# Zero products in TensorE's waits, tile ends on ScalarE, first weights in parts and gate rows a tile sooner, in an encoder layer

## Chip, core and metric

The kernel runs on one core of one Trainium2 chip. The metric is the time of one execution on the device in microseconds (us). The engines are TensorE (PE in rows: matrix products; PEld: its weight loads), VectorE (DVE), ScalarE (ACT), GpSimd (POOL) and SyncE (SP). Each runs its own queue of instructions in order. SP's queue issues the loads and POOL's queue the stores.

## What is computed

One layer of a hybrid encoder on 1024 tokens of 1024 channels, in fp32. The part that this change touches is the normalization, its modulation by `c`, and the projection to q and k:

```python
mod = jax.nn.silu(c) @ w_ada + b_ada
sh1, sc1, gt1, sh2, sc2, gt2 = jnp.split(mod[:, None, :], N_MOD, axis=-1)
h = rmsnorm(x, norm1_g) * (1.0 + sc1) + sh1
z = h @ w_in
u, v, q, k, va, gate_a, gate_b = jnp.split(z, cuts, axis=-1)
a_out = gmlp_branch(u, v, gm_v_g, gm_w_s, gm_b_s) @ w_a
b_out = window_attention_branch(q, k, va, q_norm_g, k_norm_g, attn_sink) @ w_b
merged = jax.nn.sigmoid(gate_a) * a_out + jax.nn.sigmoid(gate_b) * b_out
x = x + gt1 * (merged @ w_o)
h2 = rmsnorm(x, norm2_g) * (1.0 + sc2) + sh2
f_gate, f_up = jnp.split(h2 @ w_ffn_in, 2, axis=-1)
x = x + gt2 * ((jax.nn.silu(f_gate) * f_up) @ w_ffn_out)
```

## The kernel before

Every large product of two fp32 matrices is done as three products of split operands. A number is split into a high part (a cast to float32r, on ACT) and a low part (the number less its high part, on DVE); high by high, high by low and low by high are added up in PSUM. Weights come in units of 128 x 1024 (`raw`), whose parts are called `wh` and `wl`; three buffers of each rotate. `unit` loads one, casts it and takes the low part. The activations' parts are `hH` and `hL` (both `h` in rows).

The layer works on two halves of 512 tokens: `half(0)`, `half(1)`. Activations lie transposed, channels on the partitions, in 8 tiles of 128 channels (k = 0 to 7). Half 0 takes 640 columns, the 512 tokens and 128 more for the attention window (the halo).

*Half 0's begin* is written in program order (`in_order`), so each engine's queue follows the code. The 8 tiles of `xT` are loaded, then pair 0 of modulation rows (`ada_pair(k)`: the scale row SC1+k and the shift row SH1+k of tile k, 1 MB), then the first unit of `w_q` and of `w_kv`. Squares are taken on ACT and added up on DVE in `ss`; PE sums `ss` over the partitions (`total`), ACT takes the root, DVE the reciprocal (`rcol`), PE spreads it over the partitions in a bank (`spread`), and ACT copies the bank to `rb` (tile `ss` again). For each tile k the loop then does the following:

- DVE scales the tile by its scale column and `rb` (`x`, in rows `mid<-mid,mod,ss`).
- The shift end (`ada_end(SH1 + k)`) turns the dotted shift row into the column `sh`: one DVE operation on 128x1 (`mod<-acc_mod,cc`).
- ACT makes `hH` and the halo's high part and shifted copy, POOL the halo's low part (`mid<-mid,mid 128x128`).
- DVE dots the next tile's scale row with silu(c) (`ada_dot`, in rows `mid,acc_mod<-mid,silu_c`), makes `hL`, takes the scale end of the next tile (`mod<-acc_mod,badap,cc`) and dots the next shift row. POOL's queue stores the scaled tile (`x0d`).
- PE does 8 products of 512 columns for q with `hH` and 4 with `hL` (banks `mm`), and 10 and 5 of 256 columns for k (banks `at`).

A unit of `w_q` holds two tiles' weights and one of `w_kv` four. At each odd k below 7 the next `w_q` unit is loaded, cast and split; the second `w_kv` unit is loaded at k = 3 and split at k = 4. Behind the loop come the products for v. A scheduler sets the order of what is not `in_order`.

*Half 1* runs the same loop on activations that are ready (`h_next`) with its first units split ahead (`early`). In it the rows for the gates (GT1 and on) are brought in, each in two halves of 512 columns in the streams `hs` and `xs`: `ada_half_load` issues the loads on SP, `ada_half` dots both halves on DVE, takes the ends, and loads the next row.

Every operation recorded through the engines' wrapper has the line L76, every load L137.

## Time and profile before

| | |
|---|---|
| runs (us) | 1243.43, 1244.94, 1246.81; median 1244.94 |
| profiled execution | 1245.15 us, of which the span is 1243.3 |
| busy, of the span | PE 98%, PEld 81%, DVE 74%, ACT 46%, POOL 15% |
| granted TensorE clock, mean | 0.999 |
| idle time of PE before its column sums, for DVE's `ss` | 7.5 us, once |

The span is what the hardware profiler recorded from the first instruction to the last. A row of the timeline gives the start and the busy time in us, the engine, the line, the operation, what it writes and reads with the shape, a count of neighbours put together, and in brackets the idle time before it and what ended that. Rows of a sequence of instructions overlap a little, since an instruction starts before the one ahead has drained.

### The profile page before, as it was taken

Reading aid. Unit: us, or ns where it says so; the run is one execution under the profiler, and the core shown is the slowest. Engines: PE = TensorE matmul, PEld = TensorE weight load, DVE = VectorE, ACT = ScalarE, POOL = GpSimd, SP = SyncE. Lnnn points to the kernel's source line nnn. Section 1 sums busy time; section 2 is a strip of 40 time slices with the busy share of each in tenths; the row PEclk is TensorE's granted clock in tenths of the full one; section 3 lists DMA queues with packets and bytes.
Section 4 is the critical chain, followed back from the end, with each engine's and each line's share of the span. In section 5 each row is a group of like instructions: output and inputs, shape, how many; then the busy total and the mean of one; then the engine's idle time right before and its main releaser. Section 6 shows DMA issues by size and latency. Waiting matters only on the chain.

```text
span 1243.3 us, 15662 instructions
## 1 busy us (share of the span) xinstructions
PE 1220.3 (98%) x5634; PEld 1010.6 (81%) x5634; DVE 914.7 (74%) x1548; ACT 577.3 (46%) x938; POOL 183.6 (15%) x233
## 2 busy tenths in 40 slices
PE   6999999999999999999999999999999999999998
PEld 4888888888887787888888888888888887888887
DVE  8997884487898798966797766666766666665746
ACT  5467864267876333534554333333333335433341
POOL 1223430023432001322100001010000000010001
PEclk9999999999999999999999999999999999999999
DMA  9622258431157457777503445455554459896642
GB/s 367 254 102 81 74 193 289 145 102 52 51 174 237 164 190 251 282 261 255 201 34 119 174 149 202 153 194 200 188 212 160 170 195 376 318 349 231 199 153 102
DMA packets 77664, 236.29 MB, mean 190 GB/s; under 512 B 9361, under 2 KB 9361, under 8 KB 71570
## 3 DMA queue, kind: packets, MB, share of 16 engines
q1 hardware_dynamic: 55442, 143.00, 33.0%
q0 software_dynamic: 18688, 85.99, 19.4%
q10 hardware_dynamic: 3456, 6.29, 1.3%
q8 instruction: 44, 0.72, 0.2%
q14 instruction: 34, 0.28, 0.1%
HBM read 177.58 MB, written 57.67 MB: 189 GB/s over the span
## 4 chain that ended last, share of the span: by engine, by line
PE 71%; DVE 11%; issue 9%; DMA 4%; ACT 3%; POOL 0%; SPq 0%; ACTq 0%; DVEq 0%; POOLq 0%
PE mm L76 36%; PE at L76 35%; DVE mid L76 3%; DVE wl L76 2%; ACT wh L76 2%; DMA wo<-in_w_out_dram 1%; DMA wS<-wo 1%; DVE hs L76 1%; DMA raw<-in_w_ga_dram 1%; DMA xs<-x1sd 1%; DVE t L76 1%; DVE ws L76 1%; DVE xs L76 1%; DVE raw L76 1%; ACT lb L76 1%
## 5 line engine op out<-in xcount | busy, mean ns | idle before, releaser
L76 ACT CAST wh<-raw 128x1024 fp32r<-128x1024 f32 x155 | 162.3, 1051 | 145.0 <-PE at L76 44.5
L76 DVE TENSOR_TENSOR wl<-raw,wh 128x1024 fp32r<-128x1024 f32 x141 | 171.9, 1221 | 71.1 <-ACT wh L76 68.8
L76 PE MATMUL mm<-mid,wh 128*128 128x512 f32 x696 | 214.8, 390 | 0.3
L76 PEld LDWEIGHTS mm<-mid,wh 128*128 128x128 f32 x696 | 130.3, 188 | 28.0 <-DVE xs L76 0.6
L76 PE MATMUL at<-j,wh 128*128 128x512 f32 x464 | 143.0, 389 | 0.0
L76 PE MATMUL mm<-mid,wl 128*128 128x512 f32 x348 | 135.5, 389 | 0.5 <-POOL wl L76 0.5
L76 PE MATMUL mm<-wh,h 128*128 128x512 f32 x384 | 129.7, 399 | 1.9 <-ACT h L76 1.9
L76 PEld LDWEIGHTS at<-j,wh 128*128 128x128 f32 x464 | 86.9, 188 | 18.6 <-ACT wh L76 0.4
L76 DVE TENSOR_TENSOR wl<-ws,wh 128x1024 fp32r<-128x1024 f32 (+1 forms) x55 | 62.0, 1128 | 44.4 <-ACT wh L76 44.4
L76 PE MATMUL at<-j,wl 128*128 128x512 f32 x232 | 90.4, 390 | 0.5 <-DVE wl L76 0.5
L76 PE MATMUL mm<-j,wh 128*128 128x512 f32 x288 | 89.0, 390 | 0.3 <-ACT wh L76 0.3
L76 PE MATMUL at<-h,wh 128*128 128x512 f32 x288 | 88.9, 390 | 0.0
L76 PEld LDWEIGHTS mm<-wh,h 128*128 128x128 f32 x384 | 71.7, 189 | 16.7 <-ACT h L76 2.8
L76 PE MATMUL mm<-h,wh 128*128 128x512 f32 x272 | 84.6, 392 | 0.0
L76 ACT CAST wh<-ws 128x1024 fp32r<-128x1024 f32 (+1 forms) x55 | 53.6, 974 | 58.1 <-DVE ws L76 42.1
L76 PEld LDWEIGHTS mm<-mid,wl 128*128 128x128 f32 x348 | 65.3, 188 | 14.6 <-POOL wl L76 1.0
L76 PE MATMUL mm<-wl,h 128*128 128x512 f32 x192 | 76.0, 396 | 0.7 <-DVE wl L76 0.7
L76 PEld LDWEIGHTS mm<-j,wh 128*128 128x128 f32 x288 | 53.8, 188 | 11.7 <-ACT wh L76 0.7
L76 PEld LDWEIGHTS at<-h,wh 128*128 128x128 f32 x288 | 53.9, 188 | 11.1
L76 PEld LDWEIGHTS mm<-h,wh 128*128 128x128 f32 x272 | 50.6, 188 | 10.4
L76 ACT ACTIVATE xs<-xs 128x512 f32<-128x512 f32 x21 | 13.3, 632 | 96.8 <-DVE xs L76 96.8
L76 PE MATMUL mm<-j,wl 128*128 128x512 f32 x144 | 56.2, 390 | 0.5 <-DVE wl L76 0.5
(286 smaller groups left out, 2558.9 us busy)
## 6 DMA issues: line engine op xcount, KB each, us to landing
raw<-in_w_gate_dram SPq DMA_DIRECT2D x28, 512.0 KB, 5.1
tA<-hid POOLq DMA_DIRECT2D x11, 1024.0 KB, 4.9
tB<-hid POOLq DMA_DIRECT2D x11, 1024.0 KB, 4.9
wo<-in_w_out_dram POOLq DMA_DIRECT2D x22, 512.0 KB, 6.4
wS<-wo POOLq DMA_DIRECT2D x11, 1024.0 KB, 5.3
raw<-wS SPq DMA_DIRECT2D x44, 256.0 KB, 3.1
raw<-tB SPq DMA_DIRECT2D x44, 256.0 KB, 4.2
raw<-in_w_out_dram SPq DMA_DIRECT2D x33, 256.0 KB, 5.5
```

The source lines that it names most:

```text
L76: ins = f(*args, **kw)
```

## The change

It does four things.

- `warm(n)` issues n products of 128x512 of zeros into the first q bank, which the first real product starts afresh: 18 ahead of the column sums, 2 between these and the spread, 4 behind the openings of the k banks. The q banks are taken earlier for it.
- The loop's shift ends and scale ends go from DVE to ACT. A scale end is an activation there, with the gain as its scale and the new column `badg` (badap times the gain, one DVE operation of 128x8) as its bias. The scale end of tile 0 stays on DVE.
- The first units of `w_q` and `w_kv` are loaded in parts (512 and 512, 256 and 768 columns), with pair 1 between; casts and low parts are done in the same parts. Tile 0 is scaled in two parts straight from the spread's banks, and the copy to `rb` comes after `hH(0)`. The low part of each later `w_q` unit is taken at the even tile that needs it, after `x`, not at the odd tile before.
- Half 1 loads gate rows at k = 1 and 2 and dots them at k = 3 to 6, where it loaded at 2 and 3 and dotted at 4 to 7.

The order of PE's first instructions, before, from the column sums (`at<-ones,ss`) over the spread (`at<-ident,rcol`) and the openings of the k banks (`at<-identr,zeros`) to the first products:

```order
L76 MATMUL at_190<-ones,ss_167 128x1 x5
L76 MATMUL at_212<-ident,rcol_122 128x128 x4
L76 MATMUL at_218<-ident,rcol_122 128x128
L76 MATMUL at_229<-identr,zeros 128x512
L76 MATMUL at_230<-identr,zeros 128x512
L76 MATMUL mm_225<-wh_202,h_221 128x512
L76 MATMUL mm_225<-wl_203,h_221 128x512
```

And PE's after the change, from just behind the products of `crow`:

```order
L76 MATMUL mm_196<-identr,zeros 128x512 x18
L76 MATMUL at_218<-ones,ss_172 128x1 x5
L76 MATMUL mm_196<-identr,zeros 128x512 x2
L76 MATMUL at_239<-ident,rcol_123 128x128 x4
L76 MATMUL at_244<-ident,rcol_123 128x128
L76 MATMUL at_250<-identr,zeros 128x512
L76 MATMUL at_251<-identr,zeros 128x512
L76 MATMUL mm_196<-identr,zeros 128x512 x4
L76 MATMUL mm_196<-wh_230,h_246 128x512
L76 MATMUL mm_196<-wl_231,h_246 128x512
```

The products of zeros (`mm_196<-identr,zeros`) stand ahead of each of the three steps. DVE's order before, from the reciprocal to the `x` operation of tile 1:

```order
L76 RECIPROCAL rcol_122<-ms_196 128x5
L76 SCALAR_TENSOR_TENSOR mid_157,acc_mod<-mid_157,silu_c 128x1024
L76 TENSOR_TENSOR wl_203<-raw_159,wh_202 128x1024
L76 SCALAR_TENSOR_TENSOR mid_127<-mid_127,mod,ss_211 128x640
L76 TENSOR_SCALAR mod<-acc_mod,cc 128x1
L76 TENSOR_TENSOR wl_207<-raw_161,wh_206 128x1024
L76 SCALAR_TENSOR_TENSOR mid_209,acc_mod<-mid_209,silu_c 128x1024
L76 SCALAR_TENSOR_TENSOR h_223<-mid_127,mod,h_221 128x512
L76 SCALAR_TENSOR_TENSOR mod<-acc_mod,badap,cc 128x1
L76 SCALAR_TENSOR_TENSOR mid_209,acc_mod<-mid_209,silu_c 128x1024
L76 SCALAR_TENSOR_TENSOR mid_127<-mid_127,mod,ss_211 128x640
L76 TENSOR_SCALAR mod<-acc_mod,cc 128x1
```

DVE's after, over the same stretch, with `x` of tile 0 in parts from the banks (`at_239`, `at_244`):

```order
L76 RECIPROCAL rcol_123<-ms_224 128x5
L76 SCALAR_TENSOR_TENSOR mid_158,acc_mod<-mid_158,silu_c 128x1024
L76 SCALAR_TENSOR_TENSOR mid_128<-mid_128,mod,at_239 128x512
L76 TENSOR_TENSOR wl_231<-raw_160,wh_230 128x512
L76 SCALAR_TENSOR_TENSOR mid_128<-mid_128,mod,at_244 128x128
L76 TENSOR_TENSOR wl_234<-raw_161,wh_233 128x256
L76 SCALAR_TENSOR_TENSOR mid_164,acc_mod<-mid_164,silu_c 128x1024
L76 SCALAR_TENSOR_TENSOR h_248<-mid_128,mod,h_246 128x512
L76 SCALAR_TENSOR_TENSOR mid_164,acc_mod<-mid_164,silu_c 128x1024
L76 SCALAR_TENSOR_TENSOR mid_128<-mid_128,mod,ss_236 128x640
L76 TENSOR_TENSOR wl_231<-raw_160,wh_230 128x512
L76 TENSOR_TENSOR wl_234<-raw_161,wh_233 128x768
```

The operations of 128x1 are gone from DVE, the low part of wq stands behind the first part of `x`, and the second parts of both units stand behind `x` of tile 1. DVE's order in half 1 before, from the first gate row (`hs_2323`, `hs_2324`) to the low part of the second `w_q` unit (`wl_2278`); `wl_2244` is that of the first `w_kv` unit:

```order
L76 SCALAR_TENSOR_TENSOR hs_2323,acc_mod<-hs_2323,silu_c 128x512
L76 TENSOR_TENSOR wl_2201<-raw_2198,wh_2200 128x1024
L76 SCALAR_TENSOR_TENSOR hs_2324,part_2385<-hs_2324,silu_c 128x512
L76 TENSOR_TENSOR acc_mod<-acc_mod,part_2385 128x1
L76 TENSOR_SCALAR mod<-acc_mod,cc 128x1
L76 TENSOR_TENSOR wl_2244<-raw_2241,wh_2243 128x1024
L76 SCALAR_TENSOR_TENSOR xs_2356,acc_mod<-xs_2356,silu_c 128x512
L76 TENSOR_TENSOR wl_2278<-raw_2275,wh_2277 128x1024
```

And after; rows 1 (`xs_2335`, `xs_2336`) and 2 (`hs_2360`, `hs_2361`), the low part of the first `w_kv` unit now `wl_2277` and that of the second `w_q` unit `wl_2311`:

```order
L76 SCALAR_TENSOR_TENSOR xs_2335,acc_mod<-xs_2335,silu_c 128x512
L76 TENSOR_TENSOR wl_2234<-raw_2231,wh_2233 128x1024
L76 SCALAR_TENSOR_TENSOR xs_2336,part_2393<-xs_2336,silu_c 128x512
L76 SCALAR_TENSOR_TENSOR hs_2360,acc_mod<-hs_2360,silu_c 128x512
L76 TENSOR_TENSOR acc_mod<-acc_mod,part_2393 128x1
L76 SCALAR_TENSOR_TENSOR hs_2361,part_2427<-hs_2361,silu_c 128x512
L76 TENSOR_SCALAR mod<-acc_mod,cc 128x1
L76 TENSOR_TENSOR acc_mod<-acc_mod,part_2427 128x1
L76 TENSOR_SCALAR mod<-acc_mod,cc 128x1
L76 TENSOR_TENSOR wl_2277<-raw_2274,wh_2276 128x1024
L76 SCALAR_TENSOR_TENSOR xs_2398,acc_mod<-xs_2398,silu_c 128x512
L76 TENSOR_TENSOR wl_2311<-raw_2308,wh_2310 128x1024
```

Two gate rows instead of one stand ahead of the low part of the first `w_kv` unit, and row 3 stands where row 2 did.

The diff:

```diff
--- before.py
+++ after.py
@@ -183,6 +183,7 @@
     cc = const.tile([P, 72], F32, tag="cc", name="cc")
     bada, g1c, g2c, bsT = cc[:, :48], cc[:, 48:56], cc[:, 56:64], cc[:, 64:72]
     badap = const.tile([P, 48], F32, tag="badap", name="badap")
+    badg = small.tile([P, 16], F32, tag="badg", name="badg", bufs=1)
 
     def load_cond():
         crow = wpool.tile([P, UNIT], F32, tag="raw", name="crow")[0:1, :]
@@ -734,6 +735,14 @@
         koff = 0 if hf == 0 else NT - 1
 
 
+        def low(w, src, a, b):
+            V.tensor_tensor(w[1][:, a:b], src[:, a:b], w[0][:, a:b].bitcast(F32), op=ALU.subtract)
+
+        def warm(n):
+            for _ in range(n):
+                T.matmul(qps[0], zeros, identr.unsqueeze(1).to_broadcast([P, 4, P]), start=True,
+                         stop=True)
+
         if hf == 0:
             in_order[0] = True
             xt = [midt(F32, 1) for _ in range(3)]
@@ -746,7 +755,12 @@
             for k in range(KT):
                 load(xt[k], xT[k * P : (k + 1) * P, :640])
             r = ada_pair(0)
-            wq0, wk0 = raw_unit(w_q[0]), raw_unit(w_kv[0])
+            wq0, wk0 = (wpool.tile([P, UNIT], F32, tag="raw", name=nm("raw")) for _ in range(2))
+            load(wq0[:, :512], w_q[0][:, :512])
+            load(wk0[:, :256], w_kv[0][:, :256])
+            r1 = ada_pair(1)
+            load(wq0[:, 512:], w_q[0][:, 512:])
+            load(wk0[:, 256:], w_kv[0][:, 256:])
             cond = silu_rows(crow)
             ss = ss_tile()
             sqs = [midt(F32, 1)[:, 0, :] for _ in range(3)]
@@ -759,7 +773,10 @@
                 if k == 1:
                     silu_cond(cond)
                     V.tensor_scalar(badap, bada, 1.0, None, op0=ALU.add)
+                    V.tensor_tensor(badg[:, :8], badap[:, SC1 : SC1 + 8], g1c, op=ALU.mult)
                     build_bias(*base_bias, range(7, NH))
+            qps = [mm_bank() for _ in range(NT)]
+            warm(18)
             total = at_bank()
             for i in range(NT + 1):
                 T.matmul(total[:, i : i + 1], ss[:, i * P : (i + 1) * P], ones[:, 0:1], start=True,
@@ -770,25 +787,28 @@
             ada_end(SC1, g1c[:, 0:1])
             V.reciprocal(rcol[0], root)
             ada_dot(r[:, 1, :], SH1)
-            wq = unit(None, V, wq0)
+            wq = [wpool.tile([P, UNIT], F32R, tag=x, name=nm(x)) for x in ("wh", "wl")]
+            A.copy(wq[0][:, :512], wq0[:, :512])
             wk = [wpool.tile([P, UNIT], F32R, tag=x, name=nm(x)) for x in ("wh", "wl")]
-            A.copy(wk[0], wk0)
-            r = ada_pair(1)
+            A.copy(wk[0][:, :256], wk0[:, :256])
+            r = r1
             rb = ss_tile()
-            A.copy(rb[:, :HALF], spread(rcol[0], NT))
-            A.copy(rb[:, HALF:], spread(rcol[0][:, NT : NT + 1], 1))
+            warm(2)
+            bcs = spread(rcol[0], NT), spread(rcol[0][:, NT : NT + 1], 1)
             hH = [hid(), hid()]
             hL = [hid(), hid()]
         else:
             hH, hL = h_next
 
         nkv = NT + 1 - 2 * hf
-        qps = [mm_bank() for _ in range(NT)]
+        if hf == 1:
+            qps = [mm_bank() for _ in range(NT)]
         kbk = [at_bank() for _ in range(3)]
         if hf == 0:
             kps = [kbk[t // 2][:, (t % 2) * 256 : (t % 2 + 1) * 256] for t in range(nkv)]
             for t in range(2):
                 open_bank(kbk[t], identr, zeros)
+            warm(4)
         else:
             kps = [kbk[t][:, :256] for t in range(nkv)]
         for k in range(KT):
@@ -798,12 +818,28 @@
                 sh = mod[:, SH1 + k : SH1 + k + 1]
                 if 0 < k < KT - 1:
                     r = ada_pair(k + 1)
-                V.scalar_tensor_tensor(out=x, in0=x, scalar=mod[:, SC1 + k : SC1 + k + 1], in1=rb,
-                                       op0=ALU.mult, op1=ALU.mult)
-                ada_end(SH1 + k)
+                sc = mod[:, SC1 + k : SC1 + k + 1]
+                if k == 0:
+                    V.scalar_tensor_tensor(out=x[:, :HALF], in0=x[:, :HALF], scalar=sc, in1=bcs[0],
+                                           op0=ALU.mult, op1=ALU.mult)
+                    low(wq, wq0, 0, 512)
+                    V.scalar_tensor_tensor(out=x[:, HALF:], in0=x[:, HALF:], scalar=sc, in1=bcs[1],
+                                           op0=ALU.mult, op1=ALU.mult)
+                else:
+                    V.scalar_tensor_tensor(out=x, in0=x, scalar=sc, in1=rb, op0=ALU.mult,
+                                           op1=ALU.mult)
+                    if k % 2 == 0:
+                        low(wq, wq0, 0, UNIT)
+                A.activation(sh, acc_mod[:, SH1 + k : SH1 + k + 1], AF.Identity,
+                             bias=bada[:, SH1 + k : SH1 + k + 1])
                 A.activation(hH[k // 4][:, k % 4, :], x[:, :HALF], AF.Identity, bias=sh)
                 if k == 0:
-                    V.tensor_tensor(wk[1], wk0, wk[0].bitcast(F32), op=ALU.subtract)
+                    A.copy(rb[:, :HALF], bcs[0])
+                    A.copy(rb[:, HALF:], bcs[1])
+                    low(wk, wk0, 0, 256)
+                if k == 1:
+                    low(wq, wq0, 512, UNIT)
+                    low(wk, wk0, 256, UNIT)
                 A.activation(h4, x[:, HALF:], AF.Identity, bias=sh)
                 A.activation(x[:, HALF:], x[:, HALF:], AF.Identity, bias=sh)
                 G.tensor_tensor(hl4[:, KT + k, :], x[:, HALF:], h4.bitcast(F32), op=ALU.subtract)
@@ -813,7 +849,12 @@
                                        in1=hH[k // 4][:, k % 4, :].bitcast(F32),
                                        op0=ALU.add, op1=ALU.subtract)
                 if k < KT - 1:
-                    ada_end(SC1 + k + 1, g1c[:, k + 1 : k + 2])
+                    A.activation(mod[:, SC1 + k + 1 : SC1 + k + 2],
+                                 acc_mod[:, SC1 + k + 1 : SC1 + k + 2], AF.Identity,
+                                 scale=g1c[:, k + 1 : k + 2], bias=badg[:, k + 1 : k + 2])
+                    if k == 0:
+                        A.copy(wq[0][:, 512:], wq0[:, 512:])
+                        A.copy(wk[0][:, 256:], wk0[:, 256:])
                     ada_dot(r[:, 1, :], SH1 + k + 1)
                 store(x0d[k], x[:, :HALF])
                 if k == 7:
@@ -825,7 +866,12 @@
             if k == 4:
                 wk = unit(None, V, wk_raw)
             if k % 2 == 1 and k < KT - 1:
-                wq_next = unit(w_q[(k + 1) // 2], V)
+                if hf == 0:
+                    wq0 = raw_unit(w_q[(k + 1) // 2])
+                    wq_next = [wpool.tile([P, UNIT], F32R, tag=x, name=nm(x)) for x in ("wh", "wl")]
+                    A.copy(wq_next[0], wq0)
+                else:
+                    wq_next = unit(w_q[(k + 1) // 2], V)
             if k == 3:
                 wk_raw = raw_unit(w_kv[1])
             sts = [(hH[k // 4][:, k % 4, t * P : (t + 1) * P], hL[k // 4][:, k % 4, t * P : (t + 1) * P])
@@ -845,10 +891,10 @@
                         else:
                             T.matmul(ps, st[1], w[0][:, o : o + n], start=False,
                                      stop=bool(k == KT - 1 and last))
-            if hf == 1 and k in (2, 3):
+            if hf == 1 and k in (1, 2):
                 ada_half_load(("hs", "xs")[k % 2])
-            elif hf == 1 and k > 3:
-                ada_half(("hs", "xs")[k % 2] if k < 6 else None)
+            elif hf == 1 and 2 < k < 7:
+                ada_half(("hs", "xs")[k % 2] if k < 5 else None)
             if k % 2 == 1 and k < KT - 1:
                 wq = wq_next
         in_order[0] = False
```

## Prediction

> **What bounds the kernel now.** I read the busy shares of the engines first, then the waits of TensorE (PE in the rows), then a table of stretches of the span, then the rows of PE and of the engines it waits for. The stretches (start and end, length, and busy time of each engine with its instructions):
>
> ```profile
> core 0: us, PE busy (x) PEld busy (x) DVE busy (x) ACT busy (x) POOL busy (x), PEclk, DMA share, GB/s
> 0.00:13.60 13.60, 3.75 (x4) 1.16 (x4) 11.92 (x24) 9.53 (x13) 1.13 (x7) 1.00 0.82 291
> 13.60:21.30 7.70, 5.62 (x22) 4.84 (x22) 5.70 (x10) 3.67 (x7) 0.62 (x1) 1.00 1.02 426
> 21.30:26.20 4.90, 4.89 (x15) 4.12 (x16) 4.90 (x10) 0.98 (x3) 1.28 (x3) 1.00 1.03 432
> 26.20:45.20 19.00, 18.55 (x108) 16.14 (x107) 19.00 (x34) 8.17 (x15) 4.29 (x8) 1.00 0.92 351
> ...
> 61.50:200.00 138.50, 138.09 (x709) 115.90 (x708) 115.83 (x279) 99.84 (x221) 44.74 (x33) 1.00 0.39 133
> ```
>
> PE idles 9.85 us before 13.6 and 2.1 more before 21.3; later almost never (0.41 in the 138 us behind 61.5). So what is won by 61.5 is carried to the end if nothing gives it back. The row that decides is 26.2 to 45.2: VectorE (DVE) is busy 19.00 of 19.00 us there and PE 18.55. Both are at their limit, so an earlier start of PE is worth only what DVE can follow.
>
> PE's rows of this stage (start, busy time, operation, in brackets the idle time before and its releaser), and at the end two of a later place where PE has been busy for long:
>
> ```profile
> 2.39 3.75 PE L76 MATMUL at<-crow,ones 1*128 1x512 f32 x4 [2.39 <-DMA crow<-in_c_dram]
> 13.65 2.29 PE L76 MATMUL at<-ones,ss 128*128 128x1 f32 x10 [7.52 <-DVE ss L76]
> 16.62 2.48 PE L76 MATMUL at<-ident,rcol 128*128 128x128 f32 x10 [0.67 <-DVE rcol L76]
> ...
> 21.31 0.79 PE L76 MATMUL mm<-wh,h 128*128 128x512 f32 x1 [1.36 <-ACT h L76]
> 21.90 0.63 PE L76 MATMUL mm<-wl,h 128*128 128x512 f32 x1
> 22.32 0.63 PE L76 MATMUL mm<-wh,h 128*128 128x512 f32 x1
> ...
> 26.15 0.28 PE L76 MATMUL at<-wh,h 128*128 128x256 f32 x1
> ...
> 28.14 0.40 PE L76 MATMUL mm<-wh,h 128*128 128x512 f32 x1
> 28.38 0.39 PE L76 MATMUL mm<-wl,h 128*128 128x512 f32 x1
> ...
> 45.22 0.39 PE L76 MATMUL at<-wl,h 128*128 128x256 f32 x1 [0.47 <-DVE wl L76]
> ...
> 52.25 0.50 PE L76 MATMUL mm<-wh,h 128*128 128x512 f32 x1 [0.52 <-ACT h L76]
> ...
> 61.41 0.40 PE L76 MATMUL mm<-wh,h 128*128 128x512 f32 x1
> ...
> 561.78 0.95 PE L76 MATMUL at<-ones,ss 128*128 128x1 f32 x8
> ...
> 568.16 1.05 PE L76 MATMUL at<-ident,rcol 128*128 128x128 f32 x8
> ```
>
> The first real product starts at 21.31, and products of 512 columns follow each other every 0.42 us; from about 26.0 they follow every 0.24. PE thus runs at half rate for its first 4.7 us of dense work, although the column PEclk says 1.00. The sums (10 in 2.29) and the spread of the reciprocals (10 in 2.48) are slow too: behind dense work 8 take 0.95 and 1.05. Now ScalarE (ACT) and DVE on the way to 21.31, and at two later places:
>
> ```profile
> 18.70 0.75 ACT L76 COPY ss<-at 128x512 f32<-128x512 f32 x2 [0.58 <-PE at L76]
> 20.53 0.72 ACT L76 ACTIVATE h<-mid,mod 128x512 fp32r<-128x512 f32 x1 [1.08 <-DVE mod L76]
> ```
>
> ```profile
> 15.08 0.22 DVE L76 SCALAR_TENSOR_TENSOR mod<-acc_mod,badap,cc 128x1 f32<-128x1 f32 x1
> 16.28 0.19 DVE L76 RECIPROCAL rcol<-ms 128x5 f32<-128x5 f32 x1 [0.98 <-ACT ms L76]
> ...
> 19.49 0.89 DVE L76 SCALAR_TENSOR_TENSOR mid<-mid,mod,ss 128x640 f32<-128x640 f32 x1 [0.77 <-ACT ss L76]
> 20.29 0.21 DVE L76 TENSOR_SCALAR mod<-acc_mod,cc 128x1 f32<-128x1 f32 x1
> 20.41 1.22 DVE L76 TENSOR_TENSOR wl<-raw,wh 128x1024 fp32r<-128x1024 f32 x1
> ...
> 37.12 0.42 DVE L76 SCALAR_TENSOR_TENSOR mod<-acc_mod,badap,cc 128x1 f32<-128x1 f32 x1
> 37.46 1.21 DVE L76 SCALAR_TENSOR_TENSOR mid<-mid,silu_c 128x1024 f32<-128x1024 f32 x1
> ...
> 43.95 1.22 DVE L76 TENSOR_TENSOR wl<-raw,wh 128x1024 fp32r<-128x1024 f32 x1
> ```
>
> **The change, part by part.**
>
> *Zero products.* The 18 stand ahead of the sums and start when the products of `crow` end (2.39 + 3.75 = 6.14). At half rate they take 18 x 0.42 = 7.6 us and end by 13.8; if the rate doubles after 4.7 us, as it did behind 21.31, they end near 12.4. The sums wait for DVE until 13.65, so the idle 7.52 covers them; without a faster rate the cost is 0 to 0.15. The sums then take 10/8 of 0.95 at most, 1.15 taken for 2.29.
>
> The Trainium skill, "TensorE: Matmul & The Clock Gate", Part 1, has the array at half rate until a window of about 3.4 us has been busy, the window running freely, and lets it fall back after an idle one; the 4.7 us of the trace agree as one window and the rest of another. By that rule the 1.2 us between 12.4 and 13.6 are too short to close it.
>
> *Reciprocals.* The sums end 1.15 sooner, but DVE takes the reciprocal only after the scale dot and its end, which finish at 15.08 + 0.22 = 15.30. So it starts at 15.33 instead of 16.28: 0.95 won. The spread's first four blocks took 16.62 to 18.67, 2.05; at full rate about 1.05: 1.0 won. The copy of the spread by ACT (18.70 to 19.49 with its hand-over, 0.75 to 0.79) leaves the path, because tile 0 is scaled from the bank: 0.77 won. First x operation: 19.49 - 0.95 - 1.0 - 0.77 = 16.77. It has 512 columns, about 0.7; the shift end goes to ACT ahead of it (0.2, as on DVE, while ACT waits). The first product starts at 16.77 + 0.7 + 0.8 (20.53 to 21.31) = 18.3, 3.0 sooner. The 2 and 4 zero products and the bank openings keep PE busy until then, worth 0 to 0.5 (they could stand in the way by one product).
>
> *First weights in parts.* The low part of wq (17.49 in the old order, within DVE's wait) now comes after x(0): it is hidden before and on DVE's path after. The price of halves:
>
> ```profile
> L76 DVE TENSOR_TENSOR wl<-ru,wh 128x512 fp32r<-128x512 f32 x11 | 7.6, 689 | 5.0 <-ACT wh L76 5.0
> ```
>
> Its mean is 0.69; less the overlap of 0.08 between neighbours is 0.61, two make 1.22. The parts of wk (256 + 768) cost one more fixed start, 0.09 (0 to 0.2), x(0) in parts 0.13 (0 to 0.2). The two loads go out in halves and pair 1 goes between them; the DMA queues are full there (shares 1.02 and 1.03), so some 256 KB change places, and all of them are used microseconds after they land: 0, and up to 0.5 if a cast waits.
>
> *Ends on ACT.* A shift end takes 0.12 of DVE from start to start (20.29 to 20.41). A scale end takes 0.34 (37.12 to 37.46), of which about 0.2 is a hold: it ends with this operation of GpSimd (POOL) at 37.52:
>
> ```profile
> 36.97 0.55 POOL L76 TENSOR_TENSOR mid<-mid,mid 128x128 fp32r<-128x128 f32 x1 [0.84 <-ACT mid L76]
> ```
>
> The Trainium skill, "SBUF — State Buffer", "Who interferes with whom", has a VectorE operation with two SBUF inputs and a GpSimd one lock each other out for a whole instruction; the 0.42 beside a usual 0.22 agrees, and by that rule the hold passes to DVE's next operation.
>
> I take the hold to stay. Five ends of each kind stand between x(0) and wk's second unit: 5 x 0.12 + 0.13 x 5 = 1.25 saved (2.25 if the hold goes). ACT gets two operations of 0.2 a tile; it is under half busy in the stretch (8.17 of 19.00): 0.
>
> *Moving the low parts of later wq units* from odd to even tiles changes the order on DVE, not the count; it lets hL of the odd tile come sooner: 0 (up to 0.3 either way).
>
> *DVE's path.* From x(0) to the end of wk's second low part: 19.49 to 45.17, 25.68. After: + 1.22 + 0.09 + 0.13 - 1.25 = +0.19, 25.87. So PE's product at 45.22 starts at 16.77 + 25.87 + 0.05 = 42.7, 2.5 sooner. The cold 4.7 us had held up some 2.4 us of PE's work; most of that turns into PE's waits for hH and wl at tiles 1 to 4, late next. Behind 45.22 PE has 16.19 to 61.41, with 0.52 of wait and 0.2 of restart at 52.25. DVE has no wq low left in tile 5 and reaches hH(6) before PE: these 0.7 go. Stage end: 61.41 - 2.5 - 0.7 = 58.2, **3.2 sooner**.
>
> *Half 1's gate rows.* PE, DVE and SyncE (SP) as they are:
>
> ```profile
> 222.12 0.50 PE L76 MATMUL mm<-wl,h 128*128 128x512 f32 x1 [0.72 <-DVE wl L76]
> ```
>
> ```profile
> 209.99 0.69 DVE L76 SCALAR_TENSOR_TENSOR hs<-hs,silu_c 128x512 f32<-128x512 f32 x1 [7.87 <-DMA hs<-in_w_ada_dram]
> ...
> 212.80 1.21 DVE L76 TENSOR_TENSOR wl<-raw,wh 128x1024 fp32r<-128x1024 f32 x1
> 220.23 0.69 DVE L76 SCALAR_TENSOR_TENSOR xs<-xs,silu_c 128x512 f32<-128x512 f32 x1 [6.22 <-DMA xs<-in_w_ada_dram]
> 220.85 1.22 DVE L76 TENSOR_TENSOR wl<-raw,wh 128x1024 fp32r<-128x1024 f32 x1
> ```
>
> ```profile
> 202.57 0.96 SPq L137 DMA_DIRECT2D hs<-in_w_ada_dram  x2
> ...
> 214.04 0.33 SPq L137 DMA_DIRECT2D raw<-in_w_kv_dram  x1
> 214.46 0.86 SPq L137 DMA_DIRECT2D xs<-in_w_ada_dram  x2
> ```
>
> SP issues the second kv load at 214.04, as wk's low part (212.80) frees its raw buffer; a gate row follows, and DVE dots its first half at 220.23, ahead of the low part that PE waits for at 222.12. In the new order rows 1 and 2 both stand ahead of wk's low part: two dots and their small ends, 1.3 us. So kv goes out 1.3 later, row 3 behind it, and PE's wait grows by 0 to 1.6 (row 3 now has only itself and one load ahead, and landing took 5.8): I take **0.9 lost**. Nearer to the full 1.3 than to 0, since nothing else releases that load; a gain is excluded, since the same chain stays and only grows.
>
> *Sum.* -3.2 + 0.9 = -2.3 against the profiled execution's 1245.15 (span 1243.3 and 1.85 around it), 1242.85. The median of the runs is 1244.94, 0.2 below that execution: **1242.6**, 0.2% faster. About 0.3% (3.7 us) is what a measurement of this kernel can tell from no change.
>
> **Rivals.**
> - *More is won.* The hold by POOL falls where DVE waits (1.0), or half 1 loses nothing (0.9), or both: 1241.6 to 1240.7. For it: DVE is full, so each saved 0.2 counts five times. Against: POOL's operation is still there, and the chain in half 1 is explicit.
> - *The rate does not hold.* The zero products open it, the pause before 13.65 or the wait for the reciprocal closes it, or it is not open yet. Then only the copy (0.77) is won at x(0), and PE is at half rate behind it: stage -0.77 + 0.19 - 0.7 = -1.3, with half 1's loss -0.4: 1244.5. For it: 22 small matmuls between 13.6 and 21.3, 5.62 of 7.70 busy, did not open it. Against: the products are dense.
> - *Slower.* Half 1's row 2 lands a whole row's time after row 1 (the wait of 7.87 for row 1), at about 217.9 instead of right behind it. Wk's low part, before it at 212.80, ends at 219.8 instead of 214.01, kv and row 3 go out 5.8 later, and that is PE's loss: -3.2 + 5.8 = +2.6, 1247.5. It decides from row 2 landing some 3 us behind row 1; over 0.3% slower needs 7 us. For it: row 1 took 7.4 us from its issue (202.57) to its use (209.99). Against: SP's 0.96 us for issuing a row is all that stands between the two.
>
> **How the numbers follow.** As forecast 0.58, more 0.26, rate does not hold 0.10, slower 0.06. The range from 1239.9 to 1245.2 takes the first three with the open bounds (waits of 0.5 and 0.3, the runs' own spread of 1243.43 to 1246.81 around their median); about 0.15 is outside. Faster by over 0.3% (below 1241.2) is the lower two thirds of "more" and the edge of the forecast: 0.30. Slower by over 0.3%: 0.06. Within: 0.64.
>
> **What would show it.** Right: sums in about 1.15 and a first product of 512 near 18.3, following each other every 0.24 at once; new waits of PE for hH and wl at tiles 1 to 4; the product that waits for wk's second low part near 42.7; first v product near 58.2; the hold on another DVE operation; a wait of 1.2 to 2.2 in half 1 near 219. Wrong: half-rate products behind 18.3, PE without waits at tiles 1 to 4 (DVE then was not the bound), a cast waiting for a part's load, or half 1's wait at 0.9 or less.

## The result, and the profile after

The changed kernel takes 1247.34 us (median of 20 runs, 1245.86 to 1250.94), the kernel before 1244.47 in as many runs of the same sessions (1243.33 to 1246.92). The ratio is 1.0024, with a 95% interval of 1.0017 to 1.0031, clear of 1: slower by about 3 us, where 1242.6 was forecast. The profiled execution of the changed kernel has a span of 1246.2 us, 2.9 longer than before.

The same product can be found in both traces, since the order of PE's work behind the zero products is the same. The lead of the changed kernel at a place is how much sooner that product starts in it. Worked out so from both timelines (places by the time of before):

| place (us of before) | 21.3 | 28.1 | 45.2 | 61.4 | 230 | 420 | 600 | 800 | 1000 | 1239 |
|---|---|---|---|---|---|---|---|---|---|---|
| lead of the changed kernel (us) | 1.57 | 3.19 | 1.15 | 1.94 | 2.40 | 2.37 | 1.51 | 0.05 | -1.97 | -2.99 |

The begin gained 1.9 us, half 1 lost nothing, and at 420 us the changed kernel was still 2.4 ahead. Then it lost 5.4 us in a slow drift, in code that the change does not touch. The table of stretches, after:

```profile
core 0: us, PE busy (x) PEld busy (x) DVE busy (x) ACT busy (x) POOL busy (x), PEclk, DMA share, GB/s
0.00:13.60 13.60, 10.67 (x22) 6.37 (x22) 11.82 (x25) 9.31 (x13) 1.14 (x7) 1.00 0.83 297
13.60:21.30 7.70, 7.37 (x35) 6.37 (x36) 6.13 (x14) 3.51 (x10) 0.86 (x2) 0.78 1.03 425
...
26.20:45.20 19.00, 17.27 (x99) 14.61 (x98) 19.00 (x28) 9.99 (x21) 5.00 (x8) 1.00 0.99 378
45.20:61.50 16.30, 16.30 (x97) 14.46 (x97) 13.18 (x21) 11.46 (x26) 3.62 (x6) 1.00 0.46 164
...
600.00:1200.00 600.00, 598.40 (x2618) 489.34 (x2617) 404.47 (x554) 225.69 (x288) 36.22 (x65) 1.00 0.55 197
```

and the last of these stretches in the kernel before:

```profile
600.00:1200.00 600.00, 597.74 (x2637) 492.67 (x2636) 407.69 (x559) 227.92 (x290) 36.66 (x66) 1.00 0.56 199
```

Between 600 and 1200 us PE is busier than before (598.40 for 597.74) and gets through fewer products (2618 for 2637), at the same granted clock. There is no new wait: each product takes longer. The groups of products between 420 and 1040 us, by form (busy time, mean ns of one), first before and then after:

```profile
L76 PE MATMUL at<-j,wh 128*128 128x512 f32 x456 | 140.4, 389 | 0.0
L76 PE MATMUL mm<-mid,wh 128*128 128x512 f32 x424 | 130.9, 390 | 0.3
L76 PE MATMUL at<-h,wh 128*128 128x512 f32 x280 | 86.4, 390 | 0.0
```

```profile
L76 PE MATMUL at<-j,wh 128*128 128x512 f32 x456 | 141.8, 392 | 0.0
L76 PE MATMUL mm<-mid,wh 128*128 128x512 f32 x424 | 132.1, 392 | 0.0
L76 PE MATMUL at<-h,wh 128*128 128x512 f32 x280 | 86.4, 390 | 0.0
```

The first operand named is the one that streams through (512 columns). Products that stream `j` or `mid` take 2 to 3 ns more, those at `at<-h` nothing. From one start to the next it is 226.7 to 226.8 ns before for all three, and 229.9, 229.6 and 226.8 after (means of all such gaps under 260 ns behind 420 us).

What differs for these products is where their operands lie. The pools opened ahead of `small` keep their addresses, but the new tile `badg` (16 columns, 64 bytes a partition) stands at the front of `small`, and all that is allocated behind it moves by 64 bytes. `j`, the pool of the feed-forward part, starts at 256 modulo 512 bytes before (the remainder of its start address by 512) and at 320 after; `mid`, `h` and the weights stay.

PE at the begin, after:

```profile
13.93 1.37 PE L76 MATMUL at<-ones,ss 128*128 128x1 f32 x10 [0.99 <-DVE ss L76]
15.16 1.20 PE L76 MATMUL mm<-identr,zeros 128*128 128x512 f32 x2
16.16 2.34 PE L76 MATMUL at<-ident,rcol 128*128 128x128 f32 x10
18.15 0.83 PE L76 MATMUL at<-identr,zeros 128*128 128x512 f32 x2
...
24.95 0.50 PE L76 MATMUL mm<-wh,h 128*128 128x512 f32 x1 [0.41 <-ACT h L76]
...
30.37 0.49 PE L76 MATMUL mm<-wh,h 128*128 128x512 f32 x1 [0.61 <-ACT h L76]
...
44.08 0.38 PE L76 MATMUL at<-wl,h 128*128 128x256 f32 x1 [0.94 <-DVE wl L76]
```

The sums run fast (1.23 from first start to the next operation), the spread does not: 16.16 to 18.15, 1.99. The granted clock (the third number from the end) says why:

```profile
15.20:16.16 0.96, 0.96 (x3) 0.66 (x4) 0.60 (x3) 0.82 (x3) 0.00 (x0) 0.50 0.95 401
16.16:18.15 1.99, 1.99 (x12) 1.99 (x11) 0.81 (x3) 0.55 (x2) 0.00 (x0) 0.50 1.09 437
```

The zero products went from 0.43 to 0.23 us apart at 11.6, and the last started at 12.55 and took 0.39. After 0.99 us without work and most of the sums the clock is back at one half, from 15.0 to 18.4. That is the rival "the rate does not hold", for the spread alone.

### The profile page after: what moved, and what is told of

Its sections match the earlier page's. It is cut to its first block, busy times and chain, and to the rows that moved or that the text cites. A ratio compares the mean times of both kernels' runs of the same rounds, so it can differ in the third digit from the quotient of the medians.

```text
span 1246.2 us, 15728 instructions
## 1 busy us (share of the span) xinstructions
PE 1232.2 (99%) x5658; PEld 1015.2 (81%) x5658; DVE 914.5 (73%) x1537; ACT 581.4 (47%) x955; POOL 185.1 (15%) x233
## 4 chain that ended last, share of the span: by engine, by line
PE 84%; DVE 6%; issue 4%; DMA 4%; ACT 2%; POOL 0%; SPq 0%; DVEq 0%; ACTq 0%; POOLq 0%
PE mm L76 42%; PE at L76 42%; DMA raw<-in_w_out_dram 2%; DVE mid L76 2%; DVE wl L76 1%; DMA xs<-in_w_ada_dram 1%; ACT wh L76 1%; DVE xs L76 1%; DVE lb L76 0%; DMA wS<-wo 0%; DMA xs<-x1sd 0%; DVE ss L76 0%; ACT lb L76 0%; DVE t L76 0%; DVE h L76 0%
## 5 line engine op out<-in xcount | busy, mean ns | idle before, releaser
L76 ACT CAST wh<-raw 128x1024 fp32r<-128x1024 f32 (+2 forms) x157 | 162.4, 1038 | 140.9 <-PE at L76 46.4
L76 DVE TENSOR_TENSOR wl<-raw,wh 128x1024 fp32r<-128x1024 f32 (+2 forms) x143 | 172.2, 1206 | 71.1 <-ACT wh L76 67.6
L76 DVE TENSOR_TENSOR ol<-raw,oh 128x1024 fp32r<-128x1024 f32 x30 | 36.7, 1225 | 28.8 <-ACT oh L76 25.6
```

What stands on the lines that cost most here:

```text
L76: ins = f(*args, **kw)
```

## The experiments

Eleven kernels ran, in three sessions, each against runs of the kernel before on the same chip. Their leads over the kernel before, at the same places:

| | 28.1 | 45.2 | 61.4 | 230 | 420 | 1239 | ratio (95%) |
|---|---|---|---|---|---|---|---|
| changed kernel | 3.19 | 1.15 | 1.94 | 2.40 | 2.37 | -2.99 | 1.0024 (1.0017, 1.0031) |
| e1: badg in nsh | 3.34 | 1.29 | 2.09 | 2.96 | 3.58 | 3.32 | 0.9986 (0.9976, 0.9997) |
| e2: before, 64 B | 0.45 | -0.12 | -0.15 | 0.58 | 1.13 | -4.18 | 1.0037 (1.0023, 1.0050) |
| e3: before, 128 B | 1.05 | -0.45 | -0.45 | 0.77 | -0.50 | -7.11 | 1.0051 (1.0035, 1.0066) |
| e4: e1, 24 zeros | 4.28 | 2.23 | 3.02 | 3.35 | 3.57 | 4.13 | 0.9974 (0.9963, 0.9985) |
| e5: j alone, 64 B | 0.26 | -0.12 | -0.14 | 0.73 | 0.07 | -5.48 | 1.0037 (1.0024, 1.0051) |
| e6: e4, half 1 old | 4.39 | 2.34 | 3.14 | 4.11 | 4.59 | 5.32 | 0.9963 (0.9950, 0.9975) |
| e7: zeros alone | 2.94 | 1.45 | 1.41 | 1.83 | 2.08 | 1.14 | 0.9988 (0.9977, 0.9998) |
| e8: e4, ends on DVE | 3.78 | 0.94 | 0.91 | 1.02 | 1.28 | 1.78 | 0.9998 (0.9988, 1.0009) |
| e9: e6, attention at 256 | 4.35 | 2.30 | 3.10 | 4.34 | 4.47 | 3.90 | 0.9963 (0.9951, 0.9975) |
| e10: before, all 64 B | 1.22 | -0.27 | -0.30 | -0.32 | -0.13 | 0.45 | 0.9997 (0.9987, 1.0006) |
| e12: zeros and ends | 2.80 | 2.00 | 2.23 | 3.29 | 3.38 | 3.04 | 0.9973 (0.9963, 0.9983) |

A lead is of one profiled execution and scatters: by up to 1.2 us between places that the edit cannot reach (e2, e5 and e3 run the code of before at the begin and in half 1), so the ratios judge and the leads show where.

### Where the 64 bytes lie: e1, e2, e3

```diff
-    badg = small.tile([P, 16], F32, tag="badg", name="badg", bufs=1)
...
-    nsh = const.tile([P, 16], F32, tag="nsh", name="nsh")[:, :8]
+    nshb = const.tile([P, 16], F32, tag="nsh", name="nsh")
+    nsh, badg = nshb[:, :8], nshb[:, 8:]
```

> The changed kernel, whole, with one difference: the new 64-byte column badg takes the unused half of an existing tile (nsh), so that every buffer behind it keeps the address it had before the change (j starts at 256 modulo 512 bytes again, instead of 320). Theory A (addresses): the loss behind 420 us, some 2000 products of 512 columns that follow each other every 229.5 to 230.8 ns instead of 226.7, comes from the buffers that badg moved by 64 bytes; it goes away, the products fall back to 226.7 ns, and what is left is the gain of the begin and of half 1, some 2.2 us: about 1242.3, ratio 0.998 to before. Rival B (the longer program or the new order moves something that lasts, for example how instructions arrive or which mid buffer holds what): the pitch stays near 230 ns and the time near 1247.3, ratio 1.002.

1244.1 us against 1245.27, ratio 0.9986: the same work with the old addresses is faster than before, not slower. The drift behind 420 us is gone:

```profile
L76 PE MATMUL at<-j,wh 128*128 128x512 f32 x456 | 140.4, 389 | 0.0
L76 PE MATMUL mm<-mid,wh 128*128 128x512 f32 x420 | 129.5, 389 | 0.1
L76 PE MATMUL at<-h,wh 128*128 128x512 f32 x280 | 86.4, 390 | 0.0
```

The other way round, on the kernel before:

```diff
+    badg = small.tile([P, 16], F32, tag="badg", name="badg", bufs=1)
...
+                    V.tensor_tensor(badg[:, :8], badap[:, SC1 : SC1 + 8], g1c, op=ALU.mult)
```

> The kernel before with only badg added as its own tile (64 bytes a partition) and the one operation that fills it; no zero products, no moved ends, no parts. Theory A (addresses): pitch behind 420 us rises to about 230 ns, time + 4.5 to 5.5 us, about 1249.5. Rival B: nothing but one operation of 128x8 on VectorE, 1244.5 (+0 to 0.2).

1250.5 us against 1245.27, ratio 1.0037. Products of `j` and `mid` follow each other every 229.9 and 229.6 ns, as in the changed kernel. And with `[P, 32]`, 128 bytes:

> As the one before, with badg of 128 bytes instead of 64, so that j starts at 384 modulo 512. Theory A, if a start at a multiple of 128 bytes is good enough: 1244.5, pitch 226.7. Theory A, if it takes a multiple of 256: about 1249.5 or part of it. Rival B: 1244.5.

1252.12 us, ratio 1.0051. A multiple of 128 is no better: products of `j` follow each other every 232.7 ns, those of `mid` every 227.8. The address is shown as the cause, and rival B falls in all three.

### Which buffer: e5, e10

```diff
+            pad = ffn_ctx.enter_context(pool("pad")).tile([P, 16], F32, tag="pad", name="pad")
+            V.memset(pad, 0.0)
             jpools.append(ffn_ctx.enter_context(pool("j", 6, reuse_waits="tile")))
```

> The kernel before with 64 bytes put in front of the pool j alone (opened near 420 us) and one memset of them: j starts at 320 modulo 512 bytes, all other buffers keep their addresses. Theory A1 (a product is slower where its own moving operand starts at such an address): products that read j go from 226.7 to 229.8 ns, those that read mid stay at 226.7; some 1100 products by 2.3 to 3.2 ns, + 3.0 to 3.3 us, about 1248. Theory A2 (it is what other engines or transfers write to and read from the moved buffers that holds PE up): products that read mid rise too (229.6 in the changed kernel), + 5 us, about 1250. Rival B: neither, 1244.9.

1249.84 us, ratio 1.0037. `j` alone brings the whole loss, and the products of `mid`, which has not moved, slow down with it (229.6), so A1's "own operand" is not the whole of it. A2 gave the size but not the reason: the `mid` products that ran while no instruction or transfer touched `j` are as slow (229.8, 395 products). The order shows more. PE in e5 (start, time for two products, the first rows of blocks of 12):

```profile
441.25 0.63 PE L76 MATMUL mm<-mid,wh 128*128 128x512 f32 x2
...
444.02 0.63 PE L76 MATMUL at<-j,wh 128*128 128x512 f32 x2
...
446.78 0.63 PE L76 MATMUL mm<-h,wh 128*128 128x512 f32 x2
...
449.56 3.03 PE L76 MATMUL at<-j,t 128*128 128x512 f32 x12
...
455.20 0.61 PE L76 MATMUL at<-h,wh 128*128 128x512 f32 x2
...
457.92 0.40 PE L76 MATMUL mm<-j,wh 128*128 128x512 f32 x1
```

and in the kernel before:

```profile
441.01 0.62 PE L76 MATMUL mm<-mid,wh 128*128 128x512 f32 x2
...
443.73 0.62 PE L76 MATMUL at<-j,wh 128*128 128x512 f32 x2
...
446.45 0.62 PE L76 MATMUL mm<-h,wh 128*128 128x512 f32 x2
...
449.17 2.88 PE L76 MATMUL at<-j,t 128*128 128x512 f32 x12
```

Before, each block of 12 takes 2.72 us. In e5 a block that comes after a change between `j` and another buffer takes 2.76 to 2.78 (12 gaps of 230.2 to 230.8 ns on average for 226.7, 43 to 50 ns in all), and the block of `h` that follows `mid` takes 2.72 (455.20 to 457.92). Single starts in e5 show a settling: the 12 gaps of a `mid` block that follows `j` are 234, 231, 233, 236, 224, 231, 236, 228, 233, 231, 226 and 227 ns, and those of the `h` block that follows `mid` are 226 and 227 throughout. The same settling stands in the kernel before behind a run of small products (235, 233, 236, 224, 231, 236, 228 near 77 us).

`j` itself does not settle. Where 144 products that stream `j` follow each other without a change of buffer (569.64 to 602.69 in e5), they come every 228.9 ns from the 13th to the last, 226.7 in the kernel before. And where `h` streams and `j` is the second operand, the one that PEld loads as weights, four blocks of 12 in a row stay slow (the first and the last of them), in e5

```profile
626.38 2.96 PE L76 MATMUL mm<-h,j 128*128 128x512 f32 x12
...
634.77 2.96 PE L76 MATMUL at<-h,j 128*128 128x512 f32 x12
```

against the kernel before:

```profile
625.36 2.88 PE L76 MATMUL mm<-h,j 128*128 128x512 f32 x12
...
633.52 2.88 PE L76 MATMUL at<-h,j 128*128 128x512 f32 x12
```

That is 233.3 ns a product for 226.7 (means of the gaps). So a change of buffer is not by itself what costs. In the products that stay slow, the streamed operand and the weights lie at unlike offsets; products of `mid` on `wh` lie at like ones and are slow only while they settle behind such products. Whether it is the unlike offsets or the start at 320 can be tried by moving all of them:

```diff
-    nsh = const.tile([P, 16], F32, tag="nsh", name="nsh")[:, :8]
+    nsh = const.tile([P, 32], F32, tag="nsh", name="nsh")[:, :8]
```

> The kernel before with the tile nsh, the last one ahead of the weight buffers, 64 bytes longer: the weights, h, mid, the streams, j and all else behind it start 64 bytes later, so that mid, h and j start at 320 modulo 512 alike. The runs before showed j alone at 320 costing 4.7 us, with a settling of some ten products after each change from j to mid or h. Theory R (it is the difference between the buffers that PE reads one after the other): all moved alike, no difference, 227 ns behind 420 us, 1245.1. Theory S (a start at 320 is slow in itself): every product that reads j, mid or h is slow, + 5 to 12 us, 1250 to 1257.

1245.03 us, ratio 0.9997. `j`, `mid`, `h` and the weights all start at 320 modulo 512, and nothing is lost:

```profile
449.31 2.90 PE L76 MATMUL at<-j,t 128*128 128x512 f32 x12
...
452.04 0.62 PE L76 MATMUL mm<-mid,wh 128*128 128x512 f32 x2
...
454.76 0.62 PE L76 MATMUL at<-h,wh 128*128 128x512 f32 x2
...
457.48 0.62 PE L76 MATMUL mm<-j,wh 128*128 128x512 f32 x2
```

2.72 us a block again, and 226.7 ns in the stream of 144 and in the blocks of `h` on `j`. Theory R holds in so far as it is the difference between buffers, and S falls: a start at 320 is not slow in itself. Whether the same holds for the 128 bytes of e3, where the 144 products of `j` came every 232.4 ns, was not tried. The Trainium skill, "SBUF — State Buffer", "Operand start alignment", asks only for a start at a multiple of the element's size and says that its runs timed nothing; at such starts these runs show 4.7 us between like and unlike offsets (e5 against the kernel before). What in PE makes such products slow, and what settles behind them, was not tried.

The attention's buffers lie at 64 modulo 256 in the kernel before. Whether they cost the same:

```diff
+    G.memset(apool.tile([P, 48], F32, tag="pad", name="pad"), 0.0)
     bias = apool.tile([P, NH, 384], BF16, tag="bias", name="bias")
```

> As e6 (old addresses, 24 zero products, half 1's old timing), with 192 bytes put in front of the attention's buffers (bias, kbuf, the probabilities, v and others), which start at 64 modulo 256 in the kernel before: they start at 0 modulo 256 now. Between 60 and 360 us the kernel before has products at 231 to 236 ns too. If buffers at unlike offsets cause that: 227 there, some 1000 products by 4 to 5 ns, 4 us less than e6, about 1236. If the many small matmuls and pauses there cause it: the same as e6, 1240.2 within 1.

1240.92 us and a ratio of 0.9963, the same as e6. The products of the probabilities did get faster (`at<-pL,vt` from 231.8 to 226.6 ns from start to start), but there are 88 of that kind; the rest settles from the pauses and small products between.

### The begin: e4, e7, e8, e12

On e1, more zero products:

```diff
-            warm(18)
+            warm(24)
```

> As e1, with 24 products of zeros ahead of the column sums instead of 18. In the changed kernel PE was idle from 12.55 to 13.93 and its granted clock fell to 0.50 from 15.2 to 18.1, where the spread took 1.99 us instead of about 1.05. Theory: the pause closed the gate; six more products at 0.23 us fill it, the spread takes about 1.05, x(0) starts 1.0 to 1.3 sooner (about 16.9), and since VectorE bounds the stage the whole shift reaches the stage's end: 1.0 to 1.3 us less than e1. Rival: the clock falls there for another reason (the column sums count as idle, for instance): the spread stays at 1.99, the same time as e1.

1242.1 us, ratio 0.9974. The rows of PE and the granted clock in e4:

```profile
6.04 7.87 PE L76 MATMUL mm<-identr,zeros 128*128 128x512 f32 x24
13.90 1.28 PE L76 MATMUL at<-ones,ss 128*128 128x1 f32 x10
15.04 0.71 PE L76 MATMUL mm<-identr,zeros 128*128 128x512 f32 x2
15.85 1.35 PE L76 MATMUL at<-ident,rcol 128*128 128x128 f32 x10
```

```profile
15.20:18.15 2.95, 2.85 (x17) 2.27 (x18) 2.48 (x6) 1.66 (x5) 0.07 (x1) 1.00 1.00 408
```

Without the pause the clock stays at 1.00, the spread takes 1.11 (15.85 to 16.96), x(0) starts at 17.02, and the lead at 61.4 is 3.02 for 2.09 in e1. The median is 2.0 us below e1's, though the intervals of the two ratios overlap. The theory holds in this execution; the next run shows that 24 products are no guarantee.

The zero products alone, on the kernel before:

```diff
+            qps = [mm_bank() for _ in range(NT)]
+            warm(24)
             total = at_bank()
...
+            warm(2)
             A.copy(rb[:, :HALF], spread(rcol[0], NT))
...
+            warm(4)
```

> The kernel before with the zero products alone (24, 2 and 4), no new tile, nothing else changed. Theory: the gate is open from the sums on, x(0) starts 2.0 sooner (0.95 by the reciprocal, 1.0 by the spread), at 17.5; VectorE then needs its 25.7 us as before, so PE's product that waits for wk's second low part starts at 43.2, 2.0 sooner, and the lead stays 2.0 to 2.3 to the end: 1242.9. Rival (PE's cold start was the bound, VectorE follows): the lead grows to 3.5 and more by 45.

1244.14 us, ratio 0.9988. The lead is 1.45 at 45.2 and 1.41 at 61.4; it does not grow, as VectorE's bound says. It is less than 2.0 because in this execution the clock fell after all, for part of the spread and behind it:

```profile
15.20:18.15 2.95, 2.85 (x14) 2.35 (x14) 2.60 (x6) 2.81 (x5) 0.00 (x0) 0.70 1.02 429
```

Here the zero products got fast at 9.64 and the sums came after 0.4 us without work. In e6 they got fast at 9.96, the pause was 0.2, and the clock held. It also held in e8 (below), where they got fast at 10.33 and the pause was 0.4 as here, so the length of the pause alone does not decide. The Trainium skill, "TensorE: Matmul & The Clock Gate", Part 1, says that the window which decides runs freely and that the point of change differs from run to run; the first fast product between 9.64 and 12.20 in these kernels agrees. Its table has the fall back only after an idle window of about 3.4 us; in the changed kernel 1.0 us without work did it, with the sums behind it, so for this case the measurement stands against the table.

That PE's slow start costs nothing by itself shows by chance in e10, whose begin is the code of before. In that execution the products of 512 followed each other every 0.23 us from 21.9 on, where the kernel before had 0.42:

```profile
21.59 0.50 PE L76 MATMUL mm<-wh,h 128*128 128x512 f32 x1 [1.36 <-ACT h L76]
...
26.92 0.50 PE L76 MATMUL mm<-wh,h 128*128 128x512 f32 x1 [0.52 <-ACT h L76]
...
45.49 0.39 PE L76 MATMUL at<-wl,h 128*128 128x256 f32 x1 [0.56 <-DVE wl L76]
```

The lead was 1.22 at 28.1 and -0.27 at 45.2, as much as its x(0) started later (19.77 for 19.49): PE's gain turned into waits for `hH` and `wl`, as VectorE's bound says.

On e4, the ends back on VectorE:

```diff
-                A.activation(sh, acc_mod[:, SH1 + k : SH1 + k + 1], AF.Identity,
-                             bias=bada[:, SH1 + k : SH1 + k + 1])
+                ada_end(SH1 + k)
```

(and the scale ends likewise.)

> As e4 with the shift ends and scale ends back on VectorE. Theory (VectorE bounds tiles 0 to 4): its path from x(0) to wk's second low part grows by 1.25 us, PE's lead over the kernel before at the place of 45.2 falls from 2.2 to 1.0, and at 61.4 from 3.0 to 1.8. Rival (POOL's hold goes with the ends): grows by 2.2, lead 0 to 0.1 at 45.2. Rival (ScalarE's ends delay hH): no loss.

1244.53 us, ratio 0.9998. The lead falls to 0.94 at 45.2, 1.29 less than e4, as VectorE's bound and the hold that stays had it; at 61.4 it is 0.91 and not 1.8, because the wait near 52 comes back (0.52 for `h`). The ends on ScalarE are worth 2.1 us of the stage by these two profiles.

And e7 with the ends on ScalarE added (the kernel before, `badg` in `nsh`):

```diff
-                ada_end(SH1 + k)
+                A.activation(sh, acc_mod[:, SH1 + k : SH1 + k + 1], AF.Identity,
+                             bias=bada[:, SH1 + k : SH1 + k + 1])
...
-                    ada_end(SC1 + k + 1, g1c[:, k + 1 : k + 2])
+                    A.activation(mod[:, SC1 + k + 1 : SC1 + k + 2],
+                                 acc_mod[:, SC1 + k + 1 : SC1 + k + 2], AF.Identity,
+                                 scale=g1c[:, k + 1 : k + 2], bias=badg[:, k + 1 : k + 2])
```

> The kernel before with the zero products (24, 2 and 4) and the ends on ScalarE, badg in nsh, and without the parts: the first units are loaded and split whole, the copy to rb stays ahead of x(0), half 1 is as before. By the steps of the prediction: against the zeros alone (lead over the kernel before 1.4 at the place of 45.2 and of 61.4) the ends save 1.25 on VectorE's path by 45.2 and let the wait near 52 go, so the lead is 2.7 at 45.2 and 3.3 at 61.4, as much as with the parts (2.3 and 3.1 in e6): 1240 to 1241. If the parts are worth something of their own (first products sooner): 1 us more than e6.

1242.06 us, ratio 0.9973. The leads, 2.00 and 2.23, are less than the 2.7 and 3.3 expected. In this execution the zero products became fast only at 12.20, so 24 of them ran until the sums and put these off to 14.47, 0.5 to 0.6 later than in e4 (13.90); that explains most of it at 45.2. Whether the parts are worth something is not settled by this.

### Half 1: e6

```diff
-            if hf == 1 and k in (1, 2):
+            if hf == 1 and k in (2, 3):
...
-            elif hf == 1 and 2 < k < 7:
-                ada_half(("hs", "xs")[k % 2] if k < 5 else None)
+            elif hf == 1 and k > 3:
+                ada_half(("hs", "xs")[k % 2] if k < 6 else None)
```

> As e4 (old addresses, 24 zero products) with half 1's gate rows loaded at k = 2 and 3 and dotted at 4 to 7 again, as before the change. The prediction put 0.9 us of loss on that part, the changed kernel's trace shows a wait of 0.54 instead of 0.72 there. If the part loses 0.9: 0.9 less than e4. If it is neutral: the same as e4 within 0.5, and PE's lead over the kernel before at the place of 222 us (3.3 in e4) changes by no more than 0.5.

1240.16 us, ratio 0.9963, the fastest of all, but its interval overlaps that of e4, which ran in another session. From 61.4 to 230 the lead grows by 0.97 here and by 0.33 in e4. With the code of before in half 1, e2 and e5 gain 0.73 and 0.87 over the profile of before as well, so a single profile cannot tell 0.6 there. The part brings nothing that these runs show, and may cost some tenths.

## Why the prediction was wrong, step by step

- **What failed is the step that carries the lead to the end.** The prediction says that what is won by 61.5 "is carried to the end if nothing gives it back", and its sum has no term behind half 1's gate rows: `badg` stands in the list of the change as one operation on VectorE, and the space that it takes was put at nothing without a reason. Its 64 bytes moved `j` against the weights, `mid` and `h`, and that took back 5.4 us between 420 us and the end (4.7 in e5 by the runs, and 4.7 between the ratios of e1 and of the changed kernel). No rival had it: all of them looked at 0 to 230 us.
- **The rival "slower" named nearly the time, 1247.5, by luck.** Its cause, a wait of 5.8 us in half 1, did not come (the wait is 0.54, below).
- **The forecast apart from that step** fits the runs, within a wide interval: e1, the same change at the old addresses, is 0.14% faster (0.03 to 0.24%), which is 0.4 to 3.0 us, and the forecast was 2.3.
- **The sum up to 230 us** came out right in size (2.40 for 2.3) by luck: two errors cancel, a begin worth 1.3 less, and a half 1 that was to lose 0.9 and gained 0.5 in this profile, which is no more than the scatter of a lead.
- **The spread at full rate** failed: 1.99 for 1.05, since the clock fell to one half once more; the two zero products ahead of it ran at half rate too and put its start (16.16) 0.3 behind the reciprocal. x(0) started at 18.11 for 16.77. The prediction held the 1.2 us ahead of the sums too short for that; 0.99 was enough. With the pause filled (e4) it was 17.02 and the stage won 3.0, where 3.2 was forecast.
- **The reciprocal** was to be held by the scale dot at 15.33; ScalarE's root came later (15.34 to 15.61) and it started at 15.64.
- **VectorE's path** from x(0) to wk's second low part: 25.87 forecast, 25.92 measured (18.11 to 44.03, by the rows of its first and last operation below). The new waits of PE at tiles 1 to 4, 0.41, 0.61, 0.18 and 0.94, were named, and the wait near 52 went.

```profile
18.11 0.75 DVE L76 SCALAR_TENSOR_TENSOR mid<-mid,mod,at 128x512 f32<-128x512 f32 x1 [1.18 <-PE at L76]
...
42.81 1.21 DVE L76 TENSOR_TENSOR wl<-raw,wh 128x1024 fp32r<-128x1024 f32 x1
```

- **POOL's hold stayed**, as assumed, and falls on another operation of VectorE, a dot of 1.48 instead of 1.21 beside POOL's 0.50:

```profile
36.31 1.48 DVE L76 SCALAR_TENSOR_TENSOR mid<-mid,silu_c 128x1024 f32<-128x1024 f32 x1
```

```profile
36.22 0.50 POOL L76 TENSOR_TENSOR mid<-mid,mid 128x128 fp32r<-128x128 f32 x1 [0.77 <-ACT mid L76]
```

- **Half 1's 0.9 us** were mis-sized. Rows 1 and 2 do stand ahead of wk's low part, but they came sooner: DVE had row 1 6.2 us after its issue (200.62 to 206.82), not 7.4, and row 2 was there right behind it (209.19). The wait that was to grow to 1.2 to 2.2 is smaller:

```profile
219.76 0.50 PE L76 MATMUL mm<-wl,h 128*128 128x512 f32 x1 [0.54 <-DVE wl L76]
```

## What to carry to other kernels

A new tile has a second cost beside its instructions: it moves every buffer allocated behind it. Here TensorE is the bound for a millisecond, and 2 to 3 ns a product added up to more than the change won. Put small tiles into space that is already there (as in e1), or ahead of all operands that PE reads, so that they move together (as in e10), and look at the mean time of one product far from the edit before believing a lead at the begin. When idle time of PE is filled with products to hold the clock, the pause that is left ahead of the next work matters beside the number of products, and too many of them put off what waits behind.

## What the runs showed that was not expected

- Products of 512 columns whose streamed operand and weights start 64 bytes apart modulo 512 follow each other every 228.9 ns (`j` streamed) or 233.3 ns (`j` as weights) for 226.7, and those behind them need ten products to settle: 4.7 us a run (e5). At 128 bytes it is 6.8 us (e3). With all of them at 320 alike nothing is lost (e10, 0.9997).
- The granted clock fell to 0.50 for 3.4 us after 1.0 us without work and ten small sums, though 18 products had run before it. The first cold stretch shows as 1.00 in that column while products stand 0.43 apart; only the second shows as 0.50.
